# A transformer-like layer on one core: an own tile for each group's last sum, and the side work of the MLP's first matrix moved into the middle of its groups

## The chip, the core and the metric

The kernel runs on one core of a Trainium2 chip. The metric is the device time of one execution in microseconds (us), as the median of several runs. Engines are named as in the profile: PE (TensorE, matmuls), PEld (its weight loads), DVE (VectorE), ACT (ScalarE), POOL (GpSimd, which here issues the stores) and SP (SyncE, which issues the loads).

## What is computed

One layer of a decoder, in f32, for 2048 tokens of width 1024. `mod` comes from a matrix product with the conditioning vector.

```python
h = x * (1.0 + sc1) + sh1
z = h @ w_in[l]
gate_b, gate_c, v_conv, v_pool = jnp.split(
    z, [CONV_CH, 2 * CONV_CH, 3 * CONV_CH], axis=-1)
y_conv = gate_b * _short_conv(gate_c * v_conv, conv_w[l])
y_pool = _multiscale_pool(v_pool, w_pool[l], pool_scale[l])
mix = jnp.concatenate([y_conv, y_pool], axis=-1) @ w_out[l]
x = _layer_norm(DEEPNORM_ALPHA * x + (1.0 + g1) * mix, ln1_g[l], ln1_b[l])

h = x * (1.0 + sc2) + sh2
f = jnp.square(jax.nn.relu(h @ w_mlp_in[l])) @ w_mlp_out[l]
x = _layer_norm(DEEPNORM_ALPHA * x + (1.0 + g2) * f, ln2_g[l], ln2_b[l])
```

The two large products are those of the MLP: 1024 to 4096 and back.

## The kernel before

**Two halves, five stages.** The tokens are worked in two halves, b = 0 and b = 1, of T = 1024. Each goes through the input projection (`in_proj_0` or `in_proj_1`, with convolution and pooling), the output projection (`out_proj`), `up` (the MLP's first matrix, eight groups g of 512 hidden columns) and `down` (its second). In the second half `down` has a coarse part, seven products of half-size blocks for some operands, and a fine part of quarter-size blocks (matmuls of 128x256, L1166), followed by the layer norm and the stores (`Close`).

**Matrix products.** A tile of f32 is split into a high part (a cast on ScalarE, L84) and a low part (a subtraction on VectorE, L85); three matmuls, high x high, high x low and low x high (L89 to L91), make one product of f32 accuracy. On top lies a 2x2 block scheme with seven products in place of eight (`seven`): its operands and its results are sums of blocks, made on VectorE by `tt` (L96). One product is 24 matmuls of 128x512.

**A group of `up`.** Seven products (0 to 6) run one after another. Each needs a split weight operand, made from four 512 KB weight blocks (`r<-in_w`, issued by SP at L509, into a pool `r` of five tiles). Results are copied out of PSUM by ScalarE (`keep`, L1011), added to by VectorE (`add`), and passed through Relu (L1020) and Square (L1021) by `join`; `save` has POOL store each of eight results (`usum`, L1027), or stores quarter sums of them (`save_quarters`, L978 to L985) in the groups and results that the fine part reads. `c11` and, in groups from 1 on, `c22` and `c12` are the running tiles; `c11` lies in a pool `c` of two tiles and the others in a pool `o` of ten. A group ends so:

```python
for i, r in ((4, s1), (6, c12), (5, c11)):
    save(r, i)
product(6, X, False)
...
save(c21, 1)
tt(c11, c21, c11, ALU.subtract)
save(c11, 7)
```

So `c11` is handed to the store as result 5, and is then overwritten with the last sum, result 7.

**Side work in the second half's `up`.** Two kinds of other work are spread over its groups:

- *Residuals* (groups 2, 4 and 6): `rest_loads` has SP load two rows and two earlier results (L221, L1034: `o<-in_rows`, `o<-nsave`, 512 KB each) after product 1; at the end of the group `rest_of` makes four `scalar_tensor_tensor` operations (L988, L989) and two stores (`rsave`).
- *Weight quarter sums* (`quarter_sums`): four loads of 256 KB (`in_w2q`, L959), four additions of 128x512, four stores (`wquart`). There are twelve such sums in all. Four of them are made in `in_proj_1`, five in the first half's `down` (steps n = 2, 3, 6, 7 and 10) and three here, after groups 1, 3 and 5. After groups 3 and 5 result 0 of an earlier group is also loaded again (`usum`, L1473) and its quarters saved.

**What sets the order.** A tile scheduler orders the instructions of each engine from the program; each engine then takes its own in that order. `tc.issue_after(x)` puts what follows behind instruction x; `recent[0]` is the latest operand split. A tile is given a buffer of its pool as soon as one is free, so a load waits on SP for its buffer, and all loads behind it wait too.

**Start and end.** `first_group` (L377 to L413) casts the first weight block in one piece (128x512) ahead of the first shifted operand (`shifted`, L229). `Close` ends with the last 128 rows: a first scaling by the mean (L1413), in halves for the last tile, then reciprocal and root, the second scaling (L1419) in pieces of 512, 256 and 256, and the stores.

## Time and profile before

| | us |
|---|---|
| median of 3 runs | 1755.13 (1750.26 to 1757.88) |
| the profiled execution | 1756.75 |
| its span in the trace | 1755.0 |
| TensorE busy | 1725.4 |
| VectorE busy | 1390.0 |
| ScalarE busy | 887.3 |

The 1.75 us between the profiled execution's time and its span lie around the program. The mean granted clock of TensorE was 0.994.

In a timeline a row has start, duration, engine, line, operation, output<-inputs and shape; in brackets stands how long the engine was idle before it and what ended that. Names like `o<-o,ps` leave the buffer numbers out. Rows of TensorE overlap, since matmuls are pipelined: the time that one costs is the distance between starts. A window's row gives, for each engine, its busy time and number of instructions, then the clock that TensorE was granted (1.00 is full), the share of the DMA engines that was busy, and GB/s.

### The profile page before, as it was taken

What the parts mean: (1) busy time and instruction counts of PE and PEld (TensorE: products, weight loads), DVE (VectorE), ACT (ScalarE), POOL (GpSimd) and SP (SyncE); (2) the same over time, 40 slices, a digit from 0 to 9 for tenths busy, and PEclk for the clock granted to TensorE, in tenths of its full rate; (3) what the DMA queues carried; (4) which work ended last, traced back from release to release, by engine and by line L of the source; (5) the groups of instructions that cost most, each with busy time, mean ns of one, the idle gap of its engine ahead of it and who ended that gap; (6) DMA issues with size and microseconds to landing.
All of it is one profiled execution on the core that took longest, in us unless ns stands there. A gap on an engine that the chain in (4) does not pass through costs nothing.

```text
span 1755.0 us, 22936 instructions
## 1 busy us (share of the span) xinstructions
PE 1725.4 (98%) x8142; PEld 1448.3 (83%) x8142; DVE 1390.0 (79%) x1840; ACT 887.3 (51%) x1206; POOL 270.3 (15%) x483
## 2 busy tenths in 40 slices
PE   9999999999999999999999999999998989999998
PEld 8888888888888888888888878878787778999886
DVE  7897798787767786679787888687768678988897
ACT  5323368554544655345663345764444445777351
POOL 0222220123222010100001110112222221000020
PEclk9999999999999999999999999999999999999999
DMA  9899877788888999998765475757575779998771
GB/s 383 338 320 352 300 273 246 275 296 327 323 322 328 382 392 386 334 354 309 237 216 179 169 269 186 261 182 278 215 287 191 279 250 364 418 376 315 252 256 57
DMA packets 157427, 503.59 MB, mean 287 GB/s; under 512 B 18800, under 2 KB 19584, under 8 KB 157312
## 3 DMA queue, kind: packets, MB, share of 16 engines
q1 hardware_dynamic: 107712, 328.56, 51.7%
q0 software_dynamic: 49600, 173.58, 25.8%
q8 instruction: 63, 1.03, 0.2%
q14 instruction: 52, 0.43, 0.1%
HBM read 344.24 MB, written 157.82 MB: 286 GB/s over the span
## 4 chain that ended last, share of the span: by engine, by line
PE 84%; DMA 6%; issue 4%; DVE 4%; ACT 1%; POOL 0%; SPq 0%; DVEq 0%; POOLq 0%; ACTq 0%
PE ps L89 25%; PE ps L90 25%; PE ps L91 25%; PE ps L1166 7%; PE ps L413 3%; DMA r<-in_w 2%; DMA usum<-c 2%; DVE o L96 1%; PE ps L767 1%; DMA o<-hsave 1%; DMA o<-in_w2q 1%; DVE w L85 1%; POOL usum L1027 0%; DVE o L988 0%; DVE c L96 0%
## 5 line engine op out<-in xcount | busy, mean ns | idle before, releaser
L89 PE MATMUL ps<-h,w 128*128 128x512 f32 x1312 | 513.2, 392 | 15.6 <-ACT o L1011 13.9
L91 PE MATMUL ps<-h,w 128*128 128x512 f32 x1312 | 511.8, 391 | 3.7 <-DVE w L85 3.7
L90 PE MATMUL ps<-h,w 128*128 128x512 f32 x1312 | 512.4, 391 | 0.0
L89 PE MATMUL ps<-h,h 128*128 128x512 f32 (+1 forms) x936 | 362.7, 388 | 0.0
L91 PE MATMUL ps<-h,h 128*128 128x512 f32 (+1 forms) x936 | 362.7, 387 | 0.0
L90 PE MATMUL ps<-h,h 128*128 128x512 f32 (+1 forms) x936 | 362.5, 387 | 0.0
L84 ACT CAST h<-r 128x1024 fp32r<-128x1024 f32 (+1 forms) x202 | 205.4, 1021 | 271.5 <-PE ps L90 79.6
L89 PEld LDWEIGHTS ps<-h,w 128*128 128x128 f32 x1312 | 247.6, 189 | 69.9 <-ACT o L1011 16.0
L91 PEld LDWEIGHTS ps<-h,w 128*128 128x128 f32 x1312 | 247.7, 189 | 56.1 <-DVE w L85 4.5
L90 PEld LDWEIGHTS ps<-h,w 128*128 128x128 f32 x1312 | 247.7, 189 | 51.6 <-DVE h L85 0.3
L85 DVE TENSOR_TENSOR h<-r,h 128x1024 fp32r<-128x1024 f32 (+1 forms) x202 | 238.5, 1185 | 63.6 <-ACT h L84 63.3
L84 ACT CAST w<-r 128x1024 fp32r<-128x1024 f32 x156 | 163.9, 1051 | 200.8 <-PE ps L90 192.7
L85 DVE TENSOR_TENSOR w<-r,w 128x1024 fp32r<-128x1024 f32 x156 | 190.4, 1221 | 69.5 <-ACT w L84 68.8
L91 PEld LDWEIGHTS ps<-h,h 128*128 128x128 f32 x936 | 175.8, 188 | 36.0
L89 PEld LDWEIGHTS ps<-h,h 128*128 128x128 f32 x936 | 175.8, 188 | 35.9
L90 PEld LDWEIGHTS ps<-h,h 128*128 128x128 f32 x936 | 175.8, 188 | 35.5
L85 DVE TENSOR_TENSOR h<-w,h 128x1024 fp32r<-128x1024 f32 x130 | 159.5, 1227 | 8.1 <-ACT h L84 7.9
L84 ACT CAST h<-w 128x1024 fp32r<-128x1024 f32 x130 | 136.3, 1049 | 13.3 <-POOL w L1096 5.0
L96 DVE TENSOR_TENSOR o<-o,o 128x512 f32<-128x512 f32 (+2 forms) x156 | 121.4, 782 | 6.8 <-DMA o<-hsave 4.6
L96 DVE TENSOR_TENSOR o<-o,ps 128x512 f32<-128x512 f32 (+1 forms) x150 | 96.0, 650 | 37.5 <-PE ps L91 32.6
L1166 PEld LDWEIGHTS ps<-h,h 128*128 128x128 f32 x1008 | 121.1, 192 | 0.1
L1166 PE MATMUL ps<-h,h 128*128 128x256 f32 x1008 | 121.1, 283 | 0.0
(174 smaller groups left out, 1539.3 us busy)
## 6 DMA issues: line engine op xcount, KB each, us to landing
r<-usum SPq DMA_DIRECT2D x88, 512.0 KB, 6.1
w<-w2sum SPq DMA_DIRECT2D x64, 512.0 KB, 5.8
r<-in_w SPq DMA_DIRECT2D x60, 512.0 KB, 6.1
usum<-o POOLq DMA_DIRECT2D x56, 512.0 KB, 4.3
r<-uquart SPq DMA_DIRECT2D x42, 512.0 KB, 7.4
o<-in_w SPq DMA_DIRECT2D x72, 256.0 KB, 5.8
usum<-c POOLq DMA_DIRECT2D x34, 512.0 KB, 5.7
w2sum<-o POOLq DMA_DIRECT2D x64, 256.0 KB, 5.7
```

The costliest lines, as they stand in the source:

```text
L84: high = nc.scalar.copy(hi, src)
L85: return high.ins, nc.vector.tensor_tensor(lo, src, hi.bitcast(F32), op=ALU.subtract).ins
L89: nc.tensor.matmul(ps, whi, xhi, start=first, stop=False, skip_group_check=goes_on)
L90: nc.tensor.matmul(ps, whi, xlo, start=False, stop=False, skip_group_check=goes_on)
L91: nc.tensor.matmul(ps, wlo, xhi, start=False, stop=last, skip_group_check=goes_on)
L96: done = nc.vector.tensor_tensor(out_, a, b_, op=op)
L413: nc.tensor.matmul(ps[m, h], wt[:, w : w + P], A[k][p // 2][:, hs], start=k == 0 and p == 0, stop=k == KD - 1 and p == 2)
L767: nc.tensor.transpose(ps[:, t * P : t * P + P], R[4 * h + t][:, k * P : k * P + P], ident)
L1166: nc.tensor.matmul(ps, a[:, us], w[:, gs], start=not begun, stop=hf == 1 and g == 3 and a is ul, skip_group_check=True)
```

## The change

Five edits.

1. **`up`, the last sum** gets a tile `s7` of its own from the pool `o`; `c11` is no longer overwritten.
2. **`up`, side work.** A generator `aside` replaces `rest_loads` and the code after the groups. Its loads are issued after result 0 is saved (in group 1 after product 3), its arithmetic after product 3 and `c22 = keep(Z)`, behind the latest split. Residuals stay in groups 2, 4 and 6. The weight quarter sums, with the reloaded result in groups 3 and 5, are in groups 1, 3, 5 and, new, 7.
3. **`in_proj_1`** makes two quarter sums in place of four, and the first half's `down` six in place of five (n = 11 is added). There are twelve still.
4. **`first_group`**: the first weight block's cast is in two parts of 256 columns, the second behind the first shifted operand, and its subtraction in two parts.
5. **`Close`**: the last tile's first scaling is cut into 256 and 768 columns in place of 512 and 512.

```diff
-QUARTER_SUMS = (0, 1, 0, 1, 0, 1, 0, 0)
+QUARTER_SUMS = (1, 3, 5, 7)
...
             if k == 0:
-                nc.scalar.copy(wt[:, :H], wr[:, :H])
+                nc.scalar.copy(wt[:, :Q], wr[:, :Q])
...
                     high = shifted(hi, x_, k, hs)
+                    if k == 0 and hs.start == 0:
+                        with tc.issue_after(high.ins):
+                            high = nc.scalar.copy(wt[:, Q:H], wr[:, Q:H])
+                        for c in (0, Q):
+                            tt(wt[:, H + c : H + c + Q], wr[:, c : c + Q], wt[:, c : c + Q].bitcast(F32), ALU.subtract)
...
             if not last:
-                quarter_sums(t_c, recent[0])
+                quarter_sums_after(recent[0])
                 next(groups[j])
...
             next(groups[j])
-            if not last:
-                quarter_sums(t_c, recent[0])
         next(groups[-1], None)
...
-        def rest_loads():
+        def aside():
             if fine and g in REST:
...
+                ag, ab = row(t_o(D), rows[0]), row(t_o(D), rows[1])
+                tiles = [t_o(D) for _ in REST[g]]
+                for t, r in zip(REST[g], tiles):
+                    nc.sync.dma_start(r, nsave[t])
+                yield
+                for t, r in zip(REST[g], tiles):
+                    rest_of(t, r, ag, ab)
+            elif fine and g in QUARTER_SUMS:
+                sums = quarter_sums(t_o)
+                next(sums)
+                if g in (3, 5):
+                    early = t_o()
+                    nc.sync.dma_start(early, usum[g // 2 - 1, 0])
+                yield
+                next(sums, None)
+                if g in (3, 5):
+                    save_quarters(early, QUARTERED[0], g // 2 - 1)
...
         save(c11, 0)
-        loaded = rest_loads()
+        extra = aside()
+        if g != 1:
+            next(extra, None)
         yield
...
             product(3, Z, True)
             c22 = keep(Z)
+            if g == 1:
+                next(extra, None)
+            with tc.issue_after(recent[0]):
+                next(extra, None)
...
-        tt(c11, c21, c11, ALU.subtract)
-        save(c11, 7)
-        if loaded:
-            with tc.issue_after(recent[0]):
-                for t, r in zip(REST[g], loaded[2:]):
-                    rest_of(t, r, *loaded[:2])
+        s7 = t_o()
+        tt(s7, c21, c11, ALU.subtract)
+        save(s7, 7)
...
-            if b == 0 and n in (2, 3, 6, 7, 10):
-                quarter_sums(t_c, ready[1][1])
+            if b == 0 and n in (2, 3, 6, 7, 10, 11):
+                quarter_sums_after(ready[1][1])
...
-                self.tile = (t, mv, z, halves if last else [slice(0, D)])
+                self.tile = (t, mv, z, [slice(0, Q), slice(Q, D)] if last else [slice(0, D)])
```

`quarter_sums_after` issues the four loads at once and puts the additions behind the instruction that it is given, as `quarter_sums` did with loads and all. Line numbers in the changed kernel are other: the residuals are L996 and L997 there, the rows of `nsave` L1047, the weight loads L514, the quarter loads L961.

**VectorE at the boundary from group 4 to group 5 of the second half.** The `c_10496` is group 4's `c11`, `c_10783` group 5's; `o_10545` and `o_10547` are the residuals of group 4. Before:

```order
L96 TENSOR_TENSOR c_10496<-o_10718,c_10496 128x1024
L85 TENSOR_TENSOR w_10865<-r_10828,w_10864 128x1024
L96 TENSOR_TENSOR o_10731<-c_10496 128x256 x2
L96 TENSOR_TENSOR o_10731<-o_10731,c_10496 128x256
L96 TENSOR_TENSOR c_10783<-c_10783,ps_10790 128x512
L96 TENSOR_TENSOR o_10731<-c_10496,o_10731 128x256
L988 SCALAR_TENSOR_TENSOR o_10545<-o_10545,o_10541 128x1024
L988 SCALAR_TENSOR_TENSOR o_10547<-o_10547,o_10541 128x1024
L989 SCALAR_TENSOR_TENSOR o_10545<-o_10543,o_10545 128x1024
L989 SCALAR_TENSOR_TENSOR o_10547<-o_10543,o_10547 128x1024
L96 TENSOR_TENSOR c_10783<-c_10783,ps_10803 128x512
L85 TENSOR_TENSOR w_10898<-r_10747,w_10897 128x1024
```

After, the same residuals (now `o_10545` and `o_10546`) in the middle of group 4, where `w_10658` is the split for product 5, `w_10697` that for product 6, `w_10755` that for the next group's product 0, and `o_10615` is `c22`:

```order
L85 TENSOR_TENSOR w_10658<-r_10459,w_10657 128x1024
L996 SCALAR_TENSOR_TENSOR o_10545<-o_10545,o_10541 128x1024
L997 SCALAR_TENSOR_TENSOR o_10545<-o_10543,o_10545 128x1024
L996 SCALAR_TENSOR_TENSOR o_10546<-o_10546,o_10541 128x1024
L96 TENSOR_TENSOR o_10615<-o_10615,ps_10470 128x512
L997 SCALAR_TENSOR_TENSOR o_10546<-o_10543,o_10546 128x1024
L85 TENSOR_TENSOR w_10697<-r_10461,w_10696 128x1024
L96 TENSOR_TENSOR o_10615<-o_10615,ps_10483 128x512
L85 TENSOR_TENSOR w_10755<-r_10746,w_10754 128x1024
```

The four residual operations went from between the two halves of group 5's first addition to between two splits of group 4.

**SP, the loads around group 4's side work.** `r_10745` to `r_10748` before, and `r_10746` to `r_10749` after, are group 5's four weight blocks. Before:

```order
L509 DMA r_10745<-in_w 128x1024
L1473 DMA o_10434<-usum 128x1024
L509 DMA r_10746<-in_w 128x1024
L959 DMA o_10444<-in_w2q 128x512 x2
L959 DMA o_10445<-in_w2q 128x512 x2
L221 DMA o_10541<-in_rows 128x1024
L221 DMA o_10543<-in_rows 128x1024
L1034 DMA o_10545<-nsave 128x1024
L1034 DMA o_10547<-nsave 128x1024
L509 DMA r_10747<-in_w 128x1024
L509 DMA r_10748<-in_w 128x1024
```

After:

```order
L514 DMA r_10746<-in_w 128x1024
L514 DMA r_10747<-in_w 128x1024
L514 DMA r_10748<-in_w 128x1024
L221 DMA o_10541<-in_rows 128x1024
L221 DMA o_10543<-in_rows 128x1024
L1047 DMA o_10545<-nsave 128x1024
L1047 DMA o_10546<-nsave 128x1024
L514 DMA r_10749<-in_w 128x1024
```

The weight quarters and the reloaded result left this place, and the residuals' loads stand behind three of the next group's weight blocks instead of two.

**VectorE in `in_proj_1`.** `w_8276` before, and `w_8272` after, is the split of the same weight operand (a sum of blocks of the input projection's weights). Before, it stood behind the long shifted additions of the pooling (L268) and L272:

```order
L268 TENSOR_TENSOR o_8247<-o_7889 128x1039
L96 TENSOR_TENSOR o_7979<-o_7979,o_7980 128x1024
L268 TENSOR_TENSOR o_8249<-o_8247 128x1037
L96 TENSOR_TENSOR o_8171<-o_8171,ps_8219 128x512
L268 TENSOR_TENSOR o_8251<-o_8249 128x1033
L96 TENSOR_TENSOR o_8172<-o_8172,ps_8232 128x512
L272 SCALAR_TENSOR_TENSOR o_8253<-o_8251,o_7889 128x1024
L96 TENSOR_TENSOR r_8174<-r_8174,r_8173 128x1024
L96 TENSOR_TENSOR o_7890<-o_7979,o_8253 128x512
L85 TENSOR_TENSOR w_8276<-r_8173,w_8275 128x1024
```

After, it stands ahead of them:

```order
L85 TENSOR_TENSOR w_8272<-r_8169,w_8271 128x1024
L334 SCALAR_TENSOR_TENSOR o_7989<-o_7900,vecs,o_7989 128x1024
L96 TENSOR_TENSOR o_7989<-o_7989,o_7990 128x1024
L268 TENSOR_TENSOR o_8243<-o_7899 128x1039
L85 TENSOR_TENSOR w_8302<-r_8266,w_8301 128x1024
L96 TENSOR_TENSOR o_8167<-o_8167,ps_8215 128x512
L268 TENSOR_TENSOR o_8245<-o_8243 128x1037
```

That split went ahead of seven rows of the pooling and of the input projection's sums.

More of the change, by code (lines that the diff above doesn't have):

```diff
@@ L380, in first_group @@
                     nc.scalar.copy(wt[:, :H], wr[:, :H])
-                tt(wt[:, H:], wr[:, :H], wt[:, :H].bitcast(F32), ALU.subtract)
+                    tt(wt[:, H:], wr[:, :H], wt[:, :H].bitcast(F32), ALU.subtract)
                 for x_, hs in zip(a, halves):
                     high = shifted(hi, x_, k, hs)
+                    if k == 0 and hs.start == 0:
[3 more added lines that the diff above has]
+                            tt(wt[:, H + c : H + c + Q], wr[:, c : c + Q], wt[:, c : c + Q].bitcast(F32), ALU.subtract)
                     if k:
@@ L992, in tile_hybrid_layer, with quarter_sums, quarter_sums_after @@
     quarters = [(n, hf, p) for n in (2, 0, 1) for hf in range(2) for p in halves]
-    def quarter_sums(tiles, after):
+    def quarter_sums(tiles):
         n, hf, p = quarters.pop(0)
+        return sum_block([w2q[n, i, hf] for i in range(4)], wquart[n, hf], tiles, p)
+    def quarter_sums_after(after):
+        sums = quarter_sums(t_c)
+        next(sums)
         with tc.issue_after(after):
-            sum_blocks([w2q[n, i, hf] for i in range(4)], wquart[n, hf], tiles, [p])
+            next(sums, None)
     def sum_out(g, tiles):
@@ L1027, in save @@
                 nc.gpsimd.dma_start(usum[g, i], r)
-        def rest_loads():
+        def aside():
             if fine and g in REST:
-                loaded = [row(t_o(D), rows[0]), row(t_o(D), rows[1])]
-                for t in REST[g]:
-                    loaded.append(t_o(D))
-                    nc.sync.dma_start(loaded[-1], nsave[t])
-                return loaded
+                ag, ab = row(t_o(D), rows[0]), row(t_o(D), rows[1])
[7 more added lines that the diff above has]
+                sums = quarter_sums(t_o)
+                next(sums)
+                if g in (3, 5):
+                    early = t_o()
+                    nc.sync.dma_start(early, usum[g // 2 - 1, 0])
+                yield
+                next(sums, None)
+                if g in (3, 5):
+                    save_quarters(early, QUARTERED[0], g // 2 - 1)
         product(0, X, True)
@@ L1470, in mlp @@
                 pass
-            if b and g in (3, 5):
-                c11 = t_o()
-                nc.sync.dma_start(c11, usum[g // 2 - 1, 0])
-                with tc.issue_after(recent[0]):
-                    save_quarters(c11, QUARTERED[0], g // 2 - 1)
-            for _ in range(QUARTER_SUMS[g] if b else 0):
-                quarter_sums(t_o, recent[0])
             for make, src, dst, p in sums[:HALF_SUMS[g]]:
```

23 lines of the change are left out of this document (13 added, 10 removed).

## Prediction

> **What bounds the kernel now.** I read the page first, then the waits of TensorE, then its busy time in windows of 50 us, and last the timeline around the longest stall.
>
> The page's busy times:
> ```profile
> PE 1725.4 (98%) x8142; PEld 1448.3 (83%) x8142; DVE 1390.0 (79%) x1840; ACT 887.3 (51%) x1206; POOL 270.3 (15%) x483
> ```
> TensorE is the bound: all that a new order of work can give back is the time that it stands still or runs slowly. Its waits (who waited, for whom, us in total, times, longest):
> ```profile
> PE ps L89 <- ACT o L1011: 13.9, 4, 5.2
> PE ps L91 <- DVE w L85: 3.7, 1, 3.7
> PE ps L89 <- DVE o L96: 1.7, 2, 1.2
> PE ps L413 <- ACT h L229: 0.7, 1, 0.7
> ```
> The windows say where. Columns: us, busy time and count of PE, PEld, DVE, ACT and POOL, granted clock, DMA share, GB/s:
> ```profile
> 1000.00:1050.00 50.00, 46.27 (x197) 37.83 (x196) 42.98 (x48) 21.85 (x29) 5.40 (x9) 0.97 0.68 232
> 1200.00:1250.00 50.00, 50.00 (x222) 41.40 (x222) 34.72 (x46) 23.67 (x29) 14.08 (x23) 1.00 0.69 257
> 1250.00:1300.00 50.00, 47.84 (x212) 39.30 (x211) 39.95 (x56) 22.60 (x26) 14.51 (x23) 1.00 0.70 249
> 1300.00:1350.00 50.00, 44.40 (x188) 35.73 (x187) 33.72 (x42) 21.09 (x27) 12.54 (x21) 0.95 0.69 260
> 1350.00:1400.00 50.00, 48.55 (x212) 39.81 (x210) 30.91 (x44) 19.82 (x23) 12.47 (x20) 0.99 0.73 273
> 1400.00:1450.00 50.00, 44.75 (x188) 36.30 (x187) 37.04 (x45) 25.00 (x29) 9.91 (x16) 0.93 0.67 235
> 1450.00:1500.00 50.00, 50.00 (x243) 42.32 (x242) 41.65 (x43) 28.56 (x30) 6.80 (x11) 1.00 0.98 373
> ```
> An undisturbed window holds 222 matmuls, so one takes 50 / 222 = 0.225 us. The four windows from 1250 to 1450, in which the second half's `up` runs, lack 10 + 34 + 10 + 34 = 88 matmuls: 88 x 0.225 = **19.8 us**. The window at 1000, in `in_proj_1`, lacks 25: **5.6 us**. Part of each is the clock, as the longest stall shows:
> ```profile
> 1341.73 0.39 PE L91 MATMUL ps<-h,w 128*128 128x512 f32 x1
> 1347.14 0.80 PE L89 MATMUL ps<-h,w 128*128 128x512 f32 x1 [5.02 <-ACT o L1011]
> 1348.16 0.63 PE L91 MATMUL ps<-h,w 128*128 128x512 f32 x1
> 1351.53 0.39 PE L90 MATMUL ps<-h,w 128*128 128x512 f32 x1
> ```
> After 5 us of standing, matmuls last 0.63 instead of 0.39 until about 1351.5; the windows' counts hold that loss already. The Trainium skill ("TensorE: Matmul & The Clock Gate", Part 1) has the clock halved after an idle window of some 3.4 us; the trace agrees, and by that rule a stall that is only shortened below this length gives back its slow matmuls as well.
>
> Why it stands there, on VectorE (start, us; in brackets the idle time before and its cause):
> ```profile
> 1315.46 1.23 DVE L96 TENSOR_TENSOR r<-r,r 128x1024 f32<-128x1024 f32 x1 [7.57 <-DMA r<-in_w]
> 1334.20 1.23 DVE L96 TENSOR_TENSOR c<-o,c 128x1024 f32<-128x1024 f32 x1 [3.66 <-DMA usum<-c]
> 1337.48 0.68 DVE L96 TENSOR_TENSOR c<-c,ps 128x512 f32<-128x512 f32 x1
> 1338.42 2.35 DVE L988 SCALAR_TENSOR_TENSOR o<-o,o 128x1024 f32<-128x1024 f32 x2
> 1340.69 2.35 DVE L989 SCALAR_TENSOR_TENSOR o<-o,o 128x1024 f32<-128x1024 f32 x2
> 1342.96 0.68 DVE L96 TENSOR_TENSOR c<-c,ps 128x512 f32<-128x512 f32 x1
> ```
> and on ScalarE:
> ```profile
> 1343.67 1.06 ACT L1020 ACTIVATE c<-c 128x1024 f32<-128x1024 f32 x1 [11.57 <-DVE c L96]
> 1346.53 1.54 ACT L1011 COPY o<-ps 128x512 f32<-128x512 f32 x3
> ```
> The last sum of group 4 (1334.20) waits until the tile that it overwrites is stored. Then the four residual operations of group 4 stand between the two halves of group 5's first join (1337.48 and 1342.96), the Relu waits for the second, the copies out of PSUM stand behind the Relu, and TensorE waits for the copies.
>
> **The change, part by part.** All sums are made against the profiled execution, 1756.75 us (span 1755.0).
>
> *Two sums fewer in `in_proj_1`, one more in the first half's `down`.* The stall in the window at 1000 is the wait of 3.7 us for a split on VectorE (L85, 1011.88 here), which comes late because VectorE has hardly a gap, 42.98 us of 50 in that window:
> ```profile
> 992.62 0.69 DVE L96 TENSOR_TENSOR c<-c 128x512 f32<-128x512 f32 x1
> ...
> 997.83 0.69 DVE L96 TENSOR_TENSOR c<-c 128x512 f32<-128x512 f32 x1
> ...
> 1009.01 1.22 DVE L272 SCALAR_TENSOR_TENSOR o<-o,o 128x1024 f32<-128x1024 f32 x1
> 1011.88 1.22 DVE L85 TENSOR_TENSOR w<-r,w 128x1024 fp32r<-128x1024 f32 x1
> ```
> The four additions from 992.62 to 997.83 go: 4 x 0.69 = 2.8 us of the 3.7. The rest comes from the order: the split now stands ahead of L272 (1.22) and of long additions like it. The stall should go whole: **-5.6** (bounds: -2.8, the four additions alone, and -5.6). The sum added in `down` costs VectorE another 2.8 us there, at about 830, where it waits for TensorE anyhow:
> ```profile
> 834.25 0.69 DVE L96 TENSOR_TENSOR o<-o,ps 128x512 f32<-128x512 f32 x1 [2.58 <-PE ps L91]
> ```
> So 0 while that slack of 2.58 lasts; 2.8 if it were gone.
>
> *Own tile for the last sum, and residuals in the middle.* The chain above loses both links: 3.66 us of waiting, and four operations, 2.35 + 2.35 = 4.70 us, that leave the place ahead of the join. Together they are 8.4 us against a stall of 5.0, so the join comes 3.4 us ahead of need. The other three of the four waits for L1011 end on the same line, and I take the same cause for them. Over the whole stage VectorE's waits for a store, and for the weight loads, are
> ```profile
> DVE c L96 <- DMA usum<-c: 25.9, 7, 5.2
> DVE r L96 <- DMA r<-in_w: 20.9, 5, 7.6
> ```
> I take all of it: **-19.8**. What is late next is `r<-in_w`, the second row: it gives VectorE 7.57 us of idleness ahead of 1315.46, of which TensorE felt little: its waits for DVE o L96 are 1.7 in all, 1.2 the longest, which leaves 0.5 for the other. In the first half, where the last sum gets its own tile as well, TensorE has none of these waits: the idle time of the four windows, 2.2 + 5.6 + 1.4 + 5.2 = 14.4 us, is the whole 13.9 of the L1011 row and the 0.5. So 0 there.
>
> *The new place of the residuals.* They stand in VectorE's queue behind the split for product 5 and ahead of the split for product 6. Whoever waits for their loads holds that split, and TensorE behind it. The loads' time to landing in the view of their line:
> ```profile
> DMA to landing us min/median/max: 11.8/13.2/14.0
> ```
> Two weight loads, on SP, between which they would now be issued:
> ```profile
> 1297.96 0.33 SPq L509 DMA_DIRECT2D r<-in_w  x1
> 1302.22 0.33 SPq L509 DMA_DIRECT2D r<-in_w  x1
> ```
> When they are needed follows from ScalarE's first copy of group 5's first product:
> ```profile
> 1326.99 0.56 ACT L1011 COPY c<-ps 128x512 f32<-128x512 f32 x1
> ```
> That copy can come once half the product is done (12 matmuls, 2.7 us), and group 4's product 6 is the one before it (24 matmuls, 5.4 us), so product 6 starts about 1326.99 - 2.7 - 5.4 = 1318.9. Ahead of it are needed the residuals (4.70), one half join (0.68) and the split (1.22): 6.6 us, so the loads must be there by 1312.3. Issued between 1297.96 and 1302.22 and landing 13.2 later they come at 1311.2 to 1315.4: from 1.1 us early to 3.1 late; 14.0 makes 3.9. Three groups: 0 to 11.7 us. No weight quarters share their burst any longer (they are in other groups now), which speaks for the early end: I take **+1**. The Trainium skill ("DMA: Bandwidth & Descriptors", Anatomy of one DMA) fits a transfer as 2.0 us plus bytes at 436 GB/s; four loads of 512 KB alone would by that estimate land in about 7 us, and this term would be 0. The row of 11.8 disagrees, because other queues' transfers run beside them.
>
> *Quarter sums in the middle, and one in group 7.* Four additions (0.69 us each) and, in groups 3 and 5, four shorter ones on quarter tiles move from the boundary between groups into a stretch in which VectorE is idle 10 to 19 us in 50 (rows 1250 to 1400). Cost 0. Group 7's sum is new there: 1 MB read and 1 MB written just ahead of the coarse `down`, where the row 1450 shows DMA busy at 0.98 and 373 GB/s: at that rate 2.1 MB / 373 = 5.6 us if every byte delays TensorE, 0 if none does. TensorE waits for nothing in that row; I take **+1**, and keep 0 to 5.6.
>
> *First cast and last scaling in two parts.* At the start TensorE waits 0.7 (the row L413 above) for L229, which stands behind the cast. A cast of half the width can bring forward half of that at most, 0.35; the next block's operand hangs on VectorE work that the change does not touch, which takes it back: 0 (to -0.35). At the end a smaller scaling stands ahead of the reciprocal:
> ```profile
> 1747.93 0.75 DVE L1413 SCALAR_TENSOR_TENSOR o<-o,mv,w 128x512 f32<-128x512 f32 x1
> 1748.60 0.16 DVE L728 RECIPROCAL mv<-mv 128x1 f32<-128x1 f32 x1
> ```
> 256 columns instead of 512 save about 0.3 us, nothing hides it: **-0.3**.
>
> Sum: -19.8 - 5.6 - 0.3 + 1 + 1 = -23.7, so 1756.75 - 23.7 = **1733.0 us**. The median of the runs, 1755.13, lies 1.6 lower, and the same difference from it gives 1731.4; I keep the profiled base, in which the stalls were counted.
>
> **Rivals.**
> *A. Only part goes.* The load of the last weight block still stands behind the residual loads on SP, and its 7.57 us of VectorE idleness may become the link that ends last once the others are gone. For it: the chain of waits runs through that load; against it: TensorE felt some 0.5 of it. If half of the 19.8 stays: 1733.0 + 9.9 = 1742.9.
> *B. The wait moves into the middle.* The residuals' loads come late in all three groups, each stall long enough to slow the clock: 3.9 idle and, as in the row 1300 (34 x 0.225 = 7.7 lost, 50.00 - 44.40 = 5.6 of it idle), 2.1 of slow matmuls, 6.0 x 3 = 18.0: 1733.0 - 1.0 + 18.0 = 1750.0, no change. It decides once landing passes 1312.3 - 1302.22 = 10.1 us, if the loads are issued that late, or 14.3, if as early as 1297.96. The Trainium skill ("TensorE: Matmul & The Clock Gate", Architectural detail) calls VectorE's queue strictly in order, which speaks for B; the trace agrees, in that the join at 1342.96 stood behind the residuals.
> *C. Slower: the `o` buffers run short.* A group of the second half now takes twelve `o` tiles (eleven before), with ten buffers. Copies out of PSUM already wait for them:
> ```profile
> ACT o L1011 <- DMA uquart<-o: 11.6, 4, 5.4
> ```
> If each of the seven later groups waits 5.4 more on such a store and loses 2.1 to the clock, that is 7 x 7.5 = 52.5: 1733.0 + 52.5 = 1785.5. It turns to a loss where the extra wait passes 23.7 / 7 = 3.4 us a group. Against it: the new tile is stored at once, and the group's end no longer holds residual tiles.
>
> **How the numbers follow.** Forecast 0.63, A 0.20, B 0.12, C 0.05. Half a per cent, 8.8 us, is about what a measurement can tell from no change, so faster means below 1746: forecast and A, 0.83; B is the same, 0.12; C slower, 0.05. The range reaches from the lowest run without the stalls and with nothing added, 1750.26 - 25.7 = 1724.6, to A with a late group of loads, 1742.9 + 2.1 = 1745 (2.1 being one more slow stretch of the clock, from B).
>
> **What would show it.** Right: windows from 1250 on with 222 matmuls and clock 1.00, no wait for `usum<-c` on VectorE, no wait of TensorE for L1011, none at about 1009. B: the residual operations wait for `nsave`, and TensorE for a split right behind. C: copies or SP's loads wait for stores of `o` tiles. A wait for `r<-in_w` that ends in TensorE is A. Wrong altogether: no fewer stalls, or as many in the first half.

## The result, and the profile after

The changed kernel takes 1740.99 us in the median of 5 runs (1739.69 to 1743.8); the kernel before, in the same measurement, 1755.85 (1750.26 to 1757.88, 5 runs). The ratio is 0.9922, with a 95% interval of 0.9902 to 0.9941: 0.8% faster. The forecast was 1733.0, in a range of 1724.6 to 1745.0. The profiled execution took 1740.99 us, its span is 1739.2: 15.8 us less than before, where the sum had 23.7.

The busy times, to be held against the same row of before:

```profile
PE 1720.8 (99%) x8142; PEld 1444.3 (83%) x8142; DVE 1387.9 (80%) x1841; ACT 889.2 (51%) x1207; POOL 270.6 (16%) x483
```

What TensorE waited for (us in total, times, longest). The wait for the copies, L1011 before and L1024 now, is gone; what is left is short, and all of it but the start of the program (L127, and L418, which was L413 before) lies in other places than before:

```profile
PE ps L91 <- DVE w L85: 4.7, 5, 1.5
PE ps L89 <- ACT h L84: 1.2, 1, 1.2
...
PE ps L89 <- DVE o L96: 1.0, 2, 0.6
PE ps L90 <- DVE h L85: 0.8, 1, 0.8
PE ps L1194 <- ACT o L1204: 0.7, 1, 0.7
PE ps L418 <- ACT h L229: 0.7, 2, 0.4
```

The windows that lacked matmuls before. The first is whole again, the four of `up` hold 218, 219, 213 and 211 in place of 212, 188, 212 and 188, and the clock is full; the one at 1200, whole before, now lacks eight:

```profile
1000.00:1050.00 50.00, 50.00 (x223) 41.40 (x222) 43.23 (x49) 24.45 (x32) 5.39 (x9) 1.00 0.65 225
1200.00:1250.00 50.00, 48.46 (x214) 39.62 (x213) 38.28 (x51) 24.26 (x30) 12.92 (x21) 1.00 0.67 237
1250.00:1300.00 50.00, 49.38 (x218) 40.60 (x217) 36.12 (x51) 24.33 (x31) 16.59 (x27) 1.00 0.81 298
1300.00:1350.00 50.00, 49.71 (x219) 40.66 (x218) 38.46 (x50) 19.88 (x25) 13.55 (x22) 1.00 0.74 280
1350.00:1400.00 50.00, 48.46 (x213) 39.68 (x213) 38.42 (x46) 26.11 (x31) 10.41 (x17) 1.00 0.59 213
1400.00:1450.00 50.00, 48.02 (x211) 39.24 (x210) 35.77 (x50) 29.03 (x34) 14.75 (x24) 1.00 0.93 328
```

VectorE's longest waits in the second half's `up` (1130 to 1445) are new ones. Neither the store (`usum<-c`) nor, but for 2.3 us, the weight blocks (`r<-in_w`) are among them:

```profile
DVE o L996 <- DMA o<-nsave: 27.9, 3, 9.8
DVE o L96 <- DMA o<-in_w2q: 23.6, 6, 6.7
...
DVE r L96 <- DMA r<-in_w: 2.3, 1, 2.3
```

Where the time went can be read by stages. TensorE makes its matmuls in the same order in all kernels, and all traces hold 8142 of them, so the distance between the starts of the same two matmuls, by count, is a stage's time. Four such stages, in us of the profiled executions, for the two kernels and all experiments that follow:

| kernel | 3800 to 4300: end of the first half's `down`, start of `in_proj_1` | 4300 to 5000: `in_proj_1` | 5000 to 6550: `up` and coarse `down` | 6550 to 7000: first fine products |
|---|---|---|---|---|
| before | 113.3 | 160.9 | 367.9 | 54.0 |
| changed | 115.8 | 155.2 | 354.1 | 55.0 |
| own tile only | 113.3 | 160.8 | 362.8 | 54.0 |
| changed, no own tile | 116.4 | 155.3 | 364.6 | 58.5 |
| changed, residuals in the middle, sums at the end | 116.0 | 155.3 | 368.5 | 54.0 |
| changed, sums in the middle, residuals at the end | 115.4 | 155.3 | 355.1 | 54.4 |
| changed, residuals later | 117.3 | 155.3 | 356.3 | 55.2 |
| changed, no sum in group 7 | 117.0 | 155.3 | 356.3 | 54.0 |
| changed, sum at step 9 | 113.3 | 155.3 | 354.7 | 54.7 |
| changed, residual loads early | 115.8 | 155.3 | 348.9 | 55.0 |
| own tile, no sums in `up` | 119.9 | 160.8 | 346.2 | 54.0 |
| residual loads early, sum at step 9 | 113.4 | 155.3 | 350.2 | 55.4 |
| residual loads early, sums in `down` only for group 7's | 113.3 | 155.3 | 351.2 | 54.0 |
| all side loads early, sum at step 9 | 113.3 | 155.3 | 348.2 | 54.0 |

From before to changed the columns make +2.5, -5.7, -13.8 and +1.0, together -16.0. The rest lies in the first half's `up` (+0.8, around a stall at 317 that comes and goes among kernels with the same code there) and in the start and the end (-0.2 and -0.4). The kernel without sums in `up` (346.2) has no wait of TensorE in the third column, so what another kernel has above it there is its stalls, with the slow matmuls behind some of them: 21.7 us before, 7.9 in the changed kernel.

### The profile page after: what moved, and what is told of

Read it like the earlier page. It is cut to its first block, busy times and chain, and to the rows that moved or that the text cites. A ratio compares the mean times of both kernels' runs of the same rounds, so it can differ in the third digit from the quotient of the medians.

```text
span 1739.2 us, 22967 instructions
## 1 busy us (share of the span) xinstructions
PE 1720.8 (99%) x8142; PEld 1444.3 (83%) x8142; DVE 1387.9 (80%) x1841; ACT 889.2 (51%) x1207; POOL 270.6 (16%) x483
## 5 line engine op out<-in xcount | busy, mean ns | idle before, releaser
L96 DVE TENSOR_TENSOR o<-o,o 128x512 f32<-128x512 f32 (+2 forms) x174 | 129.6, 748 | 9.5 <-DMA o<-hsave 4.3
```

The costliest lines, as they stand in the source:

```text
L96: done = nc.vector.tensor_tensor(out_, a, b_, op=op)
```

## The experiments

### Own tile alone

```diff
-        tt(c11, c21, c11, ALU.subtract)
-        save(c11, 7)
+        s7 = t_o()
+        tt(s7, c21, c11, ALU.subtract)
+        save(s7, 7)
```

> The kernel before with one edit: the last sum of a group has its own tile. Theory (two links in one chain, the wait for the store and the four residual operations ahead of the next group's join): without the store's wait of 3.7 us the stalls of 5.0 and 5.25 us after groups 4 and 6 fall to about 1.5 us, too short for the clock to drop, and the smaller ones after groups 2 and 5 go. TensorE's wait for L1011 falls from 13.9 to about 3, and the time by 11 + 4 of clock = some 15 us, to about 1741; the stall at 1009 stays. Rival (the place of the residuals alone decides, since they stand in the queue whenever the sum comes): the waits for L1011 stay near 13.9 and the time near 1755. Besides, if the own tile makes the stall of 0.5 us at 317 in the first half, it shows here.

Measured: 1748.81 us, ratio 0.9958 (0.9944 to 0.9973). The wait for L1011 is gone as a whole, not down to 3, and yet only 5.1 us of the third column went. SP, VectorE and TensorE in group 4 of this kernel:

```profile
1299.16 1.02 SPq L1034 DMA_DIRECT2D o<-nsave  x2
1307.04 0.33 SPq L509 DMA_DIRECT2D r<-in_w  x1
```

```profile
1301.58 0.69 DVE L96 TENSOR_TENSOR o<-o 128x512 f32<-128x512 f32 x1 [4.30 <-DMA o<-in_w2q]
...
1305.80 2.35 DVE L85 TENSOR_TENSOR w<-r,w 128x1024 fp32r<-128x1024 f32 x2
1316.17 1.23 DVE L96 TENSOR_TENSOR r<-r,r 128x1024 f32<-128x1024 f32 x1 [8.02 <-DMA r<-in_w]
1317.31 0.68 DVE L96 TENSOR_TENSOR o<-o,ps 128x512 f32<-128x512 f32 x1
```

```profile
1318.05 0.80 PE L89 MATMUL ps<-h,w 128*128 128x512 f32 x1 [3.87 <-DVE o L96]
```

Read from the end: TensorE, at the start of group 4's product 6, waits for the first half of an addition (1317.31), which stands behind a weight sum, which waits 8.02 us for its block. The block was issued at 1307.04, when the first of the splits at 1305.80 had freed a buffer, behind 2 MB of residual loads; and those splits stood behind the quarter sums of group 3, which waited 4.30 us for their own loads. The chain of waits of the kernel before has the same pieces in the same order:

```profile
1293.61 7.24 DMA o<-in_w2q
...
1300.98 1.23 DVE w L85
...
1302.22 13.12 DMA r<-in_w
```

There the weight sum waited as long, 7.57 us to 1315.46 (the prediction shows the row), and TensorE came to product 6 at the same time, at 1313.91, against 1318.05 - 3.87 = 1314.18 here. What differs is VectorE's order. One half of the addition stood ahead of that wait, and TensorE waited for the other alone:

```profile
1307.21 0.68 DVE L96 TENSOR_TENSOR o<-o,ps 128x512 f32<-128x512 f32 x1
...
1316.61 0.68 DVE L96 TENSOR_TENSOR o<-o,ps 128x512 f32<-128x512 f32 x1
```

```profile
1317.34 0.50 PE L89 MATMUL ps<-h,w 128*128 128x512 f32 x1 [0.55 <-DVE o L96]
```

With the own tile the scheduler put both halves behind it, in group 4 and in group 6 (a stall of 3.60 us at 1400). No run changed that order alone, so this link is read from the traces.

The residual operations, which stand where they stood, show in one wait of TensorE, at the end of group 2. VectorE works without a gap from the first of them, at 1251.35, to the split that TensorE waits for, which stands behind them:

```profile
1257.08 2.35 DVE L85 TENSOR_TENSOR w<-r,w 128x1024 fp32r<-128x1024 f32 x2
```

```profile
1258.36 0.51 PE L91 MATMUL ps<-h,w 128*128 128x512 f32 x1 [1.80 <-DVE w L85]
```

Neither expectation holds: what stalls TensorE now is mainly the late weight block, which rival A of the prediction named and the forecast left at 0.

### No own tile

The same edit the other way round, in the changed kernel.

> The changed kernel, but the last sum goes back into the tile that is being stored. Theory (two links): the residuals no longer stand ahead of the join, so only the wait for the store is left, up to 5 us of VectorE's time per group, of which TensorE feels little (0 to 1 us a group): 1741 to 1747, VectorE's waits for usum<-c back at some 20 us. Rival (the own tile alone brought the gain): the stalls of 5 us come back, 1755. The stalls in the middle of groups 2 and 6 (1.5 us each, behind the wait for nsave) stay either way.

Measured: 1757.32 us, ratio 1.0007 (0.9995 to 1.002). The move alone brings nothing: 3.3 us less in the third column, 4.5 more in the fourth. VectorE waits for the store as before (23.9 us in `up`, 7 times), the buffers of `r` come free later, the loads of the quarters in the next group are issued later, and the sums that need them are now in the middle of VectorE's queue. In group 5 these loads go out from 1342.01 on, 13.3 us before TensorE is ready for product 6, against 16.6 us in the changed kernel, and TensorE waits 3.35 us there, at 1358. The theory's time is missed by 10 us; the rival's 1755 is near, but its stalls of 5 us did not come back. The two edits by themselves give -5.1 and -3.3 in the third column, and together -13.8.

### Which of the two moves

Both have the own tile. In the first the sums' loads and additions go back to the end of their groups, in the second the residuals' four operations.

```diff
-        if g != 1:
+        if g in REST:
             next(extra, None)
         yield
...
-            if g == 1:
-                next(extra, None)
-            with tc.issue_after(recent[0]):
-                next(extra, None)
+            if g in REST:
+                with tc.issue_after(recent[0]):
+                    next(extra, None)
...
         save(s7, 7)
+        if g not in REST:
+            next(extra, None)
+            with tc.issue_after(recent[0]):
+                next(extra, None)
```

> The changed kernel, but the weight quarter sums of groups 1, 3, 5 and 7 are loaded and made at the end of their groups, as before; residuals stay in the middle. Theory (three links: the store's wait, the residual operations ahead of the join, and the weight load that stands on SP behind quarter loads and residual loads together): the third link is back in part, VectorE waits 4 us or more for r<-in_w after groups 1, 3 and 5, and TensorE some 1 to 2 us for DVE o L96 in each: 1744 to 1747. Rival (the arithmetic ahead of the join alone was the second link): no such waits, 1741 or, without the sum in the middle of group 3, some 1 us less.

```diff
-            with tc.issue_after(recent[0]):
-                next(extra, None)
+            if g not in REST:
+                with tc.issue_after(recent[0]):
+                    next(extra, None)
...
         save(s7, 7)
+        if g in REST:
+            with tc.issue_after(recent[0]):
+                next(extra, None)
```

> The changed kernel, but the four residual operations stand at the end of groups 2, 4 and 6, as before; their loads and the sums are where the change has them. Theory (three links; the own tile and the spread loads break two): the residuals stand again ahead of the next group's join, 4.7 us, but with no store to wait for ahead of them VectorE has that much time: TensorE waits 0 to 1 us for the copies (L1011's successor), and the middle stalls of groups 2 and 6 (1.5 us each) go, because the loads have half a group more: 1737 to 1740. Rival (operations ahead of the join cost TensorE their length): 2 to 4 us of waiting for the copies at three boundaries, 1745 or more.

Measured: with the residuals moved, 1754.1 us, ratio 0.9986 (0.997 to 1.0002); with the sums moved, 1742.59, ratio 0.9929 (0.9906 to 0.9952). What TensorE waited for with the residuals moved, and what VectorE did in `up`:

```profile
PE ps L89 <- DVE o L96: 10.4, 3, 4.4
PE ps L91 <- DVE w L85: 5.4, 4, 2.1
```

```profile
DVE o L996 <- DMA o<-nsave: 32.6, 3, 11.2
...
DVE r L96 <- DMA r<-in_w: 4.3, 1, 4.3
```

The same with the sums moved:

```profile
PE ps L91 <- DVE w L85: 3.2, 4, 0.8
PE ps L89 <- DVE o L96: 2.0, 5, 0.6
```

```profile
DVE r L96 <- DMA r<-in_w: 23.2, 4, 7.3
```

Of the 8.7 us in the third column that the own tile does not bring by itself (362.8 to 354.1), 7.7 come with the sums alone (355.1). Moving the residuals without them is a loss: the residuals' loads stand on SP behind weight blocks whose buffers come free late, for the reason shown above, so that their operations wait up to 11.2 us in the middle of VectorE's queue, and `up` takes 5.7 us more than with the own tile alone (368.5 against 362.8). At the end of their groups, with no store to wait for, the residuals cost 1.0 us more than in the middle (355.1 against 354.1): there TensorE waits 0.81 us for the split behind them in each of the three groups. The late block is harmless now, though VectorE waits 7.3 us for it and both halves of the addition stand behind it: in group 4 its sum starts at 1308.98, and TensorE waits 0.41 us, until 1310.86.

Of the first run's expectations the theory's was the less wrong, but its stalls came by another way: not after groups 1, 3 and 5 for `r<-in_w` (4.3 us of those waits in all), but in groups 2, 4 and 6, behind the residuals. Of the second's, TensorE waited less than 1 us at a time in `up`, as the theory had it, but for splits and additions instead of the copies and in more places, and the time is 2.6 us above its range.

### No sums in `up` at all

The kernel before with the own tile; residuals at the end of their groups, in one place with nothing else.

```diff
-QUARTER_SUMS = (0, 1, 0, 1, 0, 1, 0, 0)
+QUARTER_SUMS = (0, 0, 0, 0, 0, 0, 0, 0)
...
-            if b == 0 and n in (2, 3, 6, 7, 10):
+            if b == 0 and n in (2, 3, 6, 7, 8, 9, 10, 11):
```

> The kernel before with the own tile and without any weight sum in up (three more in the first half's down, steps 8, 9 and 11); residuals at the end of their groups, as before. Theory (the quarter loads next to the residual loads hold up the weight block behind them on SP, and that wait is what is left once the store's wait is gone): the waits for r<-in_w of 8 us fall to 5 or less, the stalls of 4.3, 4.0 and 2.2 us in up go, and up with the coarse part takes some 350 us in place of 362.8; the time falls to 1737 plus up to 3 for the fuller down. Rival (the residual operations ahead of the join, or their loads alone, keep the stalls): up stays near 360, 1747 or above.

Measured: 1742.66 us, ratio 0.9915 (0.99 to 0.993). The third column is 346.2, the least of all; TensorE's two longest waits lie in other stages. Its waits, and VectorE's in `up`:

```profile
PE ps L91 <- DVE w L85: 4.1, 2, 3.7
PE ps L89 <- ACT w L84: 2.7, 1, 2.7
```

```profile
DVE r L96 <- DMA r<-in_w: 21.6, 6, 5.5
```

VectorE's waits for the weight blocks are 5.5 us at the longest, against 9.3 with the own tile alone, and the blocks come in time: in group 4 the sum starts at 1313.23, and TensorE gets to product 6 at 1316.38 without a wait. The first two rows are the stall at the end of `in_proj_1`, which this kernel still has, and one of 2.7 us at 897: three more sums in the first half's `down` cost 6.6 us in the first column, twice what was allowed for. This run does not part the two things that the sums do, their additions in VectorE's queue and their loads' traffic; that was not tried.

### Residuals later

```diff
-            with tc.issue_after(recent[0]):
-                next(extra, None)
+            if g not in REST:
+                with tc.issue_after(recent[0]):
+                    next(extra, None)
...
             product(5, Z, False)
+            if g in REST:
+                with tc.issue_after(recent[0]):
+                    next(extra, None)
             join(c12, Z)
```

> The changed kernel with the residual operations put behind the split for product 6 in place of that for product 5; loads unchanged. Theory (the split for product 6 is what TensorE waited for): the stalls of 1.54 us in groups 2 and 6 go, since nothing that TensorE needs within the next 5 us stands behind the wait: 1741 - 3.4 = 1737.6. Rival (the wait of up to 9.8 us for nsave is passed on to whatever stands behind it): it moves to the sums of the next group's weights and TensorE waits at the boundary, 1741.

Measured: 1747.08 us, ratio 0.9949 (0.9927 to 0.997). The wait for `nsave` is gone, but the operations themselves now stand ahead of the next group's first splits, and TensorE waits for those:

```profile
PE ps L91 <- DVE w L85: 6.7, 4, 2.3
```

The expectation fell; the rival had the place right (the boundary), but the wait that is passed on is not the one for `nsave`. At the first of these stalls (2.32 us at 1240) the queue has 4.7 us of residual operations ahead of the split, and ahead of them, until 1229.77, a wait of 6.49 us for a weight block. Which of the two makes the stall was not tried apart.

### Residual loads early

```diff
+        extra = aside()
+        if g in REST:
+            next(extra, None)
         product(0, X, True)
...
-        extra = aside()
-        if g != 1:
+        if g != 1 and g not in REST:
             next(extra, None)
```

> The changed kernel with the residuals' loads issued ahead of the group's product 0 in place of after product 1 (two places earlier among the weight loads on SP). Theory (the residuals stand in the middle of the queue and their loads come late): VectorE's wait of 9.8 us for nsave falls by the time between the loads, to some 5 us or less, TensorE's stalls of 1.54 us in groups 2 and 6 go: 1741 - 3.4 = 1737.6. Rival (whatever loads stand ahead, the next weight block comes behind them): VectorE's waits for r<-in_w grow by as much and TensorE waits at the boundary of groups in their place, 1741 or above.

Measured: 1739.39 us, ratio 0.9901 (0.9887 to 0.9916). By the times alone that can't be told from the changed kernel, whose interval overlaps; the trace tells it: 348.9 in the third column against 354.1. VectorE's waits for the residuals' loads are shorter, 7.0 us at the longest against 9.8:

```profile
DVE o L996 <- DMA uquart<-o: 13.5, 2, 7.0
DVE r L96 <- DMA r<-in_w: 11.0, 4, 3.5
DVE o L996 <- DMA o<-nsave: 5.3, 1, 5.3
```

The first row names a store, but its two waits are for `nsave` as well. In group 4 VectorE goes on at 1295.86; the load that it needs was issued at 1285.07, and these loads take 10.8 us to land by the median. The store that is named was issued at 1286.08, when the load already had its buffer. So rival C's shortage does not show here.

The rival's waits for `r<-in_w` did grow, from 2.3 to 11.0 us, and TensorE feels two of them, 0.75 us in group 2 and 1.08 in group 4, where half an addition stands behind the weight sum that waits:

```profile
1310.08 0.50 PE L89 MATMUL ps<-h,w 128*128 128x512 f32 x1 [1.08 <-DVE o L96]
```

That the column fell by 5.2 us even so, more than the 3.4 expected, has another reason: the stall of group 3's sum (0.62 us) and the one at 1433, in group 7, are gone as well, though both sums stand where they stood. How the residuals' loads of one group reach into the next was not followed.

### The sum at step 11

```diff
-            if b == 0 and n in (2, 3, 6, 7, 10, 11):
+            if b == 0 and n in (2, 3, 6, 7, 9, 10):
```

> The changed kernel with the sixth weight sum of the first half's down at step 9 in place of 11. Theory (the four additions at step 11 stand in a VectorE queue that is full from there to the second half's first split, so they delay it by their 4 x 0.69 = 2.8 us): the two stalls of 0.8 and 0.5 us at 895 and 907 go and the time falls by 2.5 us, to 1738.5. Rival (the stalls come from the other sums, or from the order in in_proj_1): they stay, 1741.

Measured: 1740.86 us, ratio 0.9914 (0.9898 to 0.9931), which the times can't tell from the changed kernel either. In the trace both stalls, at 895 and 907, are gone, and the first column is 113.3 as before: the expected 2.5 us. The span (1736.0) is 3.2 us shorter; the stall at 317 (0.8) is not there either.

### No sum in group 7

```diff
-QUARTER_SUMS = (1, 3, 5, 7)
+QUARTER_SUMS = (1, 3, 5)
...
-            if b == 0 and n in (2, 3, 6, 7, 10, 11):
+            if b == 0 and n in (2, 3, 6, 7, 9, 10, 11):
```

> The changed kernel without the weight sum in group 7; the first half's down makes seven (step 9 is added). Theory (the loads of that sum stand on SP ahead of the coarse part's operands and delay them): the stalls of 1.2 and 0.8 us at 1433 and of 0.7 us at 1490 go, 3.4 us with the slow starts: 1741 - 3.4 = 1737.6. Rival (the coarse part's operands come late for another reason, buffers or traffic): they stay, 1741, or 1743 if the additional sum in down delays the second half's first splits by another 2.8 us.

Measured: 1741.6 us, ratio 0.9921 (0.9901 to 0.9941). The three stalls at 1433 and 1490 are gone (the fourth column is 54.0 again), but 1.2 us more goes at the start of `in_proj_1`, as the rival had it, and the third column is 2.2 us longer, with a stall of 2.3 us at 1168 that the changed kernel has not and the kernel before had at half the length. What lengthens that one was not tried.

### The best of it

Early residual loads and the sum at step 9:

> The changed kernel with the two edits that helped by themselves: the residuals' loads issued ahead of product 0, and the sixth sum of the first half's down at step 9. Theory (the two stalls lie in different stages and have different causes, so their gains add): up takes some 349 us as with early loads alone, down and the start of in_proj_1 2.5 us less: 1739.4 - 2.5 = 1737, against the kernel before a ratio of about 0.989. Rival (the gains are one and the same, or noise): 1739 to 1741.

Measured: 1735.59 us, ratio 0.9881 (0.9865 to 0.9898): the gains add, as the table has it (113.4 in the first column, 350.2 in the third).

Early residual loads, and group 7's sum in `down` (steps 2, 3, 6, 7, 8, 9 and 10):

> Early residual loads, and no sum in group 7: the first half's down makes seven, at steps 2, 3, 6, 7, 8, 9 and 10. Theory (each of the three costs has its own place): the second half's up loses the waits in group 7 as well (about 2 us), the fine part's first stall (1 us) goes, and down stays free since step 11 has none: 1734 to 1736. Rival (down has no room for a seventh sum): the start of in_proj_1 gets its stalls of 2.5 us back, 1737 to 1739.

Measured: 1731.29 us, ratio 0.9856 (0.9841 to 0.9871). Seven sums have room in `down`, as long as none is at step 11.

All side loads of a group, from group 2 on, ahead of its product 0, four sums in `up`, the sixth of `down` at step 9:

```diff
+        extra = aside()
+        if g > 1:
+            next(extra, None)
         product(0, X, True)
...
-        extra = aside()
-        if g != 1:
-            next(extra, None)
...
-            if b == 0 and n in (2, 3, 6, 7, 10, 11):
+            if b == 0 and n in (2, 3, 6, 7, 9, 10):
```

> As the kernel with early residual loads and the sum at step 9, but the loads of the weight quarters and of the reloaded result are ahead of product 0 too, in all groups from 2 on. Theory (what stands in the middle of VectorE's queue is cheap when its data is there): VectorE's waits for in_w2q, 23.6 us in the changed kernel, fall below 10, the stalls of TensorE behind them in groups 3 and 5 (1.0 us and less) go: 1736. Rival (weight blocks that come behind these loads are the next to be late): waits for r<-in_w of 5 us and more in groups 3 and 5, stalls at their boundaries, 1740 or above.

Measured: 1732.19 us, ratio 0.9858 (0.9843 to 0.9873). The waits for the quarters did not fall below 10 but to 12.5, which is enough; those for weight blocks are there, as the rival had it, and TensorE feels one of them, 1.04 us in group 2 (the other wait of its row below is the one at 317):

```profile
PE ps L89 <- DVE o L96: 1.8, 2, 1.0
```

```profile
DVE r L96 <- DMA r<-in_w: 19.2, 6, 4.8
...
DVE o L96 <- DMA o<-in_w2q: 12.5, 8, 4.7
```

The last two can't be told apart; both are faster than the changed kernel by an interval that doesn't touch its own, and than the kernel before by 1.4%.

## Why the prediction was right, and where it was not

**The direction and the range** held, and so did the account of what there was to gain: the stalls of the kernel before in `up` and `in_proj_1` are gone, each of them. The time is nearer to rival A's 1742.9 than to the forecast, but not by A's course: in the changed kernel VectorE waits 2.3 us for a weight block. That the range held although two causes were priced wrongly, the residuals' operations too high and the sums' move at 0, is in part luck.

**`in_proj_1`, -5.6:** measured -5.7, in all kernels with that edit and in none without it. Whether the four additions or the new order did it was not tried apart.

**The first half's `down`, 0:** wrong, +2.5. The step read a wait of 2.58 us at 834 as cover. The sum's additions stand behind it, at 839 to 844 in the changed kernel. The queue has gaps after them, the first of 2.52 us at 855, but these move along: they are waits for ScalarE, and ScalarE itself waits for a load that comes late on SP.

```profile
854.20 1.05 ACT L84 CAST w<-r 128x1024 fp32r<-128x1024 f32 x1 [6.67 <-DMA r<-in_wins]
```

```profile
SPq L961 <- DMA wquart<-c: 5.4, 2, 3.4
```

The load, of the second half's first weight block, was issued at 848.47, against 843.57 with the sum at step 9, where ScalarE waited 3.07 us for it. Ahead of it on SP stand loads of the next sum, which wait for the stores of this one (the second row, from 838 to 852); with the sum at step 9 SP has no such wait there. Splits that stand behind the additions come later as well; the two were not tried apart. Step 9 has cover, step 11 has none (the sum at step 9).

**The own tile and the moved residuals, -19.8:** the size was right, the second cause for the most part wrong. The prediction summed 3.66 us of waiting and 4.70 us of operations against a stall of 5.0. The first is a cause: with the own tile alone the wait for the copies goes as a whole. The residual operations are a small one: left at the groups' ends they hold up a split by 1.80 us once with the own tile alone, by 0.81 us three times with the sums moved, and not at all where no sums are in `up`; and moving them to the middle gained 1.0 us in the third column, not 4.70 per stall. The larger link was the late weight block, 7.57 us of VectorE's time in the row at 1315.46, which the prediction saw, and called little because TensorE had felt 0.5 of it. It was little because half of the addition that TensorE needs stood ahead of it; in the order that comes with the own tile both halves stand behind, and TensorE waits 3.87 us. What removed that was to take the quarter sums away from the place where all side loads met, the part of the change that stood at "cost 0".

**The residuals' new place, +1, between 0 and 11.7:** measured 4.4 between the starts of the same matmuls (2.0, 0.6 and 1.9 in groups 2, 4 and 6, against the kernel without sums in `up`). The loads landed in 11.3 us by the median,

```profile
DMA to landing us min/median/max: 10.1/11.3/12.2
```

less than the 13.2 of before, as was argued, and still too late in groups 2 and 6. Group 2 in the changed kernel, on SP, VectorE and TensorE:

```profile
1215.22 0.96 SPq L1047 DMA_DIRECT2D o<-nsave  x2
```

```profile
1226.50 1.23 DVE L996 SCALAR_TENSOR_TENSOR o<-o,o 128x1024 f32<-128x1024 f32 x1 [9.77 <-DMA o<-nsave]
1231.77 1.22 DVE L85 TENSOR_TENSOR w<-r,w 128x1024 fp32r<-128x1024 f32 x1
```

```profile
1233.05 0.50 PE L91 MATMUL ps<-h,w 128*128 128x512 f32 x1 [1.54 <-DVE w L85]
```

This is the course of rival B: the wait is for `nsave`, and TensorE waits for the split behind it, 1.54 us in groups 2 and 6 and 0.29 in group 4. Its price was a quarter of what the rival had: the waits are shorter than its 3.9 us, and the clock stayed full behind them. The deadline was misread too: the prediction put the start of product 6 at 1318.9, from a copy on ScalarE, while TensorE began it at 1313.91 in the kernel before. With that start, loads issued at the early end, 1297.96, and landing in 11.3 us come 1297.96 + 11.3 - (1313.91 - 6.6) = 2.0 us late, which is near what was measured.

The Trainium skill's fit ("DMA: Bandwidth & Descriptors", Anatomy of one DMA) is given there for transfers that GpSimd issues; by the prediction's estimate from it these loads, which SP issues, would have taken about 7 us and the term been 0. The row has 10.1 at the least, so it is not borne out here. That other transfers beside them are the reason, as the prediction says, was not tried.

**The sums in the middle, 0, and group 7's, +1:** measured 0.9 (a stall of 0.6 us of waiting in group 3) and 3.5. The latter are the stalls at 1433 and 1490, which go when the sum does (no sum in group 7); the one at 1433 goes with early residual loads as well, so the sum alone does not make it. The bounds held it, 0 to 5.6.

**First cast and last scaling:** -0.2 at the 200th matmul, and -0.4 from the last matmul's start to the end of the span (8.60 before, 8.24 after), against 0 and -0.3. Neither is shown: kernels with the old end take 8.2 to 9.0 us there and those with the new one 8.0 to 9.0, and the first 200 matmuls take 44.1 to 44.7 with the old start and 43.8 to 44.5 with the new one.

**Not foreseen at all:** the stall of 1.16 us at 1169, which lies outside the windows that the prediction counted, is not there in the changed kernel (-1.6), and the one at 317 is longer (+0.8). Both vary among kernels with the same code in that place.

So of the shortfall of 7.9 us, 23.7 against 15.8, 2.5 is the step in `down`, 3.4 the residuals' place, 2.5 group 7 and 0.9 the sums, together 9.3; the stall at 1169, gone unforeseen, takes 1.6 off, and the rest is small.

## What to carry to other kernels

What a wait in an in-order queue costs depends on what stands behind it. Waits of 7.57 and 8.02 us for the same weight block cost TensorE 0.55 us with half an addition ahead of them and 3.87 us with all of it behind, and an edit that removes another wait can change that order. So each long wait has to be priced in the order of the new kernel, even where it costs nothing now. Work put into the middle of an in-order queue is free only if its data is already there, so move its loads ahead by more than their landing time, and not only the work. And a gap in a queue is cover only if it comes behind the added work, and if what ends the gap does not come later by that work as well.

## What the hardware showed

How long TensorE stood did not decide by itself whether its clock fell. With the own tile alone it waited 1.80 us at 1258, and the next 3.4 us had half the clock; without the own tile it waited 3.35 us at 1358, and the clock stayed. The windows around the first, and then the second:

```profile
1256.00:1258.70 2.70, 0.90 (x5) 0.43 (x4) 2.70 (x4) 1.47 (x2) 0.55 (x1) 1.00 0.91 352
1258.70:1262.10 3.40, 3.40 (x10) 2.66 (x9) 3.33 (x6) 2.55 (x4) 2.06 (x3) 0.50 0.90 267
```

```profile
1354.00:1358.70 4.70, 1.34 (x7) 0.81 (x5) 4.62 (x8) 0.00 (x0) 2.04 (x3) 1.00 0.93 350
1358.70:1365.00 6.30, 6.30 (x28) 5.22 (x29) 6.27 (x7) 4.13 (x4) 0.54 (x1) 1.00 0.24 95
```

The Trainium skill ("TensorE: Matmul & The Clock Gate", Part 1) has the clock fall after an idle window of some 3.4 us that runs freely, whatever the kernel does. A free-running window can let a stall of 3.35 us pass; a stall of 1.80 us that halves the clock it does not explain, and no run here does.
